# A hybrid decoder block on one core: where a scan's second output tile is finished, the order of its state products, and two output steps ahead of the last states

## The chip, the core and the metric

The kernel runs on one core of a Trainium2 chip. It is timed in device microseconds (us) from start to end of one execution. The core has engines that run side by side, each with its own queue of instructions: TensorE for matrix products (PE in the profile, with PEld for its weight loads), VectorE (DVE), ScalarE (ACT), GpSimd (POOL) and SyncE (SP), which issues most of the transfers from memory. Products land in PSUM, a small memory beside the large SBUF. An engine takes its instructions in their order; where one has to wait for another engine, all that is behind it in its queue waits too.

## What is computed

One layer of a decoder for 512 tokens of width 1024, with 16 learned tokens (the "meta" tokens) put in front. Two branches read the same normalised input: a pooling branch and a Mamba-2 branch, a scan with 8 groups of 4 heads. Each is projected back to width 1024, weighted by a gate of its own, and their sum goes through `w_o` and an MLP with a squared ReLU. The case is about the Mamba-2 branch:

```python
xbc = silu(causal_depthwise_conv(xbc, conv_w, conv_b))      # x, B and C of every group
dt = softplus(dt_raw + dt_bias)
...
cb = einsum("bclgn,bcsgn->bclsg", cf, bf)                   # C against B within a chunk
y_diag = einsum("bclsg,bclsgr,bcsgrp->bclgrp", cb, lmat, xdt)
decay_states = exp(a_cs[:, :, -1:] - a_cs)
states = einsum("bclgn,bclgr,bclgrp->bcgrpn", bf, decay_states, xdt)
# states are carried from chunk to chunk: h = chunk_decay * h + state
y_off = einsum("bclgn,bcgrpn,bclgr->bclgrp", cf, prev, exp(a_cs))
y = y_diag + y_off + xs * d_skip
y = y * silu(z)
y = y * rsqrt(mean(y * y, over the group's 256 channels) + eps) * norm_w
y_ssd = y @ w_ssd_out
h = h + (gate_pool * y_pool + gate_ssd * y_ssd) @ w_o
```

The sequence is cut into chunks of 128 tokens; the 16 meta tokens form a short chunk of their own ahead of the four others.

## The kernel before

**Precision.** Every large product is made of three: each operand is split into a high part (the cast `whi` for weights, L75) and a low part (`wlo`, the difference, L76), and high by high, high by low and low by high are added up. So each block of weights (128 x 1024) costs ScalarE a cast and VectorE a subtraction. `block()` (L81) hands out the next split block and first prepares one more, so that two lie ready ahead during the scans.

**The scan.** A loop runs over the 8 groups; I call the pass for group g round g. Within round g TensorE alternates between the scan of group g and *steps*, which are other products that keep it busy while VectorE and ScalarE work on the scan. In rounds 0 to 3, 5 and 6 the steps are the four projections of the next group's B, C and x (`xbc_tile`, tile `px`, each followed by its convolution `conv`, L344, on ScalarE and VectorE). In round 4 they are eight products of the output projection over the first eight row tiles (`out_half`), and in round 7 eight more over row tiles 8 to 13 (`out_part`, L593, tile `psp`; each is followed by a sum onto `acc` on VectorE, L597). Then, except in round 7, come the two z projections (`z_half`, tile `pz`) and, where `GATE_AT` has an entry (rounds 1, 2, 3 and 6), the product of one gate (`gate_product`, tile `pgp`).

The parts of a scan, in the order in which `scan_with` (L601) issues them:

- `turn`: B and x are turned to token-major by TensorE into PSUM (tiles `ptb`, `ptm`, `ptx`). ScalarE copies B's meta columns to `bm` and the rest to `btok`; VectorE makes the meta rows `xm`, then `xdt` (x times dt), the low part of `bm` (L449) and `xdd` (`xdt` times the decay, L450).
- `steps[0]`, then what is `held` over from the round before, then `spread` (the exponentials `eb`, L457, on ScalarE), then the function that `steps[0]` returned.
- `states`: TensorE makes the chunks' products of C and B (`pcb`, L475) and the four states (`pst`): the one of the meta chunk from `bm` and `xm` (L482), and three from `btok` and `xdd` (L484). ScalarE copies the first; VectorE carries the states on (L488, L489).
- Two more steps, between them `spans`, `decays` (ScalarE turns `abc` into decays) and `scores` (L493: VectorE multiplies `abc` by the masked products).
- `outputs`: TensorE makes `po` (L503) from the carried states and `py` (L509) from `abc` and `xdt`. More steps, `gather` (y, gated by `zt`), `squares`, and the norm's column sums (`png`, L529).

`root` turns the sums into the factor `rs` (ScalarE, L533 and L534). `finish` (L536) then does for each of the two row tiles of the group: y times the norm weight and `rs` on VectorE (L539), a cast to `yh` on ScalarE (L542), the difference `yl` on VectorE (L543), and appends the pair to `ys`, from which the output projection reads.

**Order.** The whole scan stands in a region in which TensorE, ScalarE and VectorE each issue their instructions in the order in which the code emits them. The two lists that matter at the seam of two rounds are `held`, whose entries are called behind `steps[0]` of the next round, and `steps`. At the end of a round without a gate (0, 4 and 5) the SiLU of `zt` is put into `held`; with a gate it is done at once and the gate's sigmoid (L672), which reads `pgp`, is put into `held`. `finish` comes before the next round's `turn`, except in round 4, where it is called within the scan, as in round 7.

**PSUM.** Two pools: `psa` with two buffers of 1024 columns (L59), for `px`, `pz`, `pgp`, `psp` and the like, and `psb` with four of 512 columns. A product into a buffer waits until the last reader of the buffer's former tile is done.

## Time and profile before

| | |
|---|---|
| median of 3 runs | 1022.80 us (1022.66 to 1023.13) |
| the profiled execution | 1022.52 us |
| its span, first to last instruction | 1020.8 us |
| mean granted TensorE clock | 0.997 of full speed |
| TensorE busy | 1003.9 us, 98% of the span |
| VectorE busy | 712.3 us, 70% |
| ScalarE busy | 561.5 us, 55% |
| GpSimd busy | 88.7 us, 9% |

The profile records each instruction with its line in the code, the tile it writes and those it reads, its start and its duration. For idle time it names the instruction that ended it. Matmuls are pipelined and their ends are modelled, so neighbours overlap in the record. Further views give the busy time of each engine in any stretch, with the clock that TensorE was granted in it. Times within the profile count from the start of the span.

### The profile page before, as it was taken

To read this page: it belongs to the slowest core of one execution; us is meant where nothing else is said; L and a number is where in the kernel's file an instruction comes from. 1 tells how busy PE (TensorE), PEld (TensorE's weight loads), DVE (VectorE), ACT (ScalarE), POOL (GpSimd) and SP (SyncE) were. 2 spreads that over 40 slices of the span, in tenths; PEclk is the share of its full clock that TensorE was granted. 3 is DMA by queue.
4 is the path that set the end of the run, shared out by engine and by line. 5 is a ranking of instruction groups with operands and counts; after the bars stand their busy time and mean duration, and the time that the engine had idled before them with its cause. 6 is when DMAs were issued, how large, how long until landed. Compare 5 with 4: busy or idle time off the path is not lost.

```text
span 1020.8 us, 14036 instructions
## 1 busy us (share of the span) xinstructions
PE 1003.9 (98%) x5689; PEld 873.6 (86%) x5689; DVE 712.3 (70%) x894; ACT 561.5 (55%) x789; POOL 88.7 (9%) x52
## 2 busy tenths in 40 slices
PE   9999999999999999999999999999999999999997
PEld 8889889898889998978899888888888888888886
DVE  7978586777645586767765466985776577666865
ACT  7765958595843659494244343474545455354444
POOL 0100000000000000000000001003040431413400
PEclk9999999999999999999999999999999999999999
DMA  6233232323232231323632334133323323324112
GB/s 239 71 139 103 63 121 66 125 76 131 83 124 83 83 105 62 127 83 100 206 103 84 107 101 138 68 107 141 103 81 116 113 83 123 92 95 124 42 42 83
DMA packets 29282, 105.64 MB, mean 103 GB/s; under 512 B 3296, under 2 KB 4256, under 8 KB 28192
## 3 DMA queue, kind: packets, MB, share of 16 engines
q1 hardware_dynamic: 26496, 92.75, 28.4%
q0 software_dynamic: 2000, 11.08, 3.0%
q8 instruction: 45, 0.74, 0.3%
q10 hardware_dynamic: 720, 0.91, 0.2%
q14 instruction: 21, 0.17, 0.1%
HBM read 102.55 MB, written 2.16 MB: 103 GB/s over the span
## 4 chain that ended last, share of the span: by engine, by line
PE 84%; ACT 9%; DVE 6%; issue 1%; DMA 0%; SPq 0%; ACTq 0%
PE pf L100 6%; PE pf L99 6%; PE pf L101 6%; PE px L157 5%; PE px L158 5%; PE px L160 5%; PE alpha L1063 3%; PE alpha L1064 3%; PE alpha L1065 3%; PE pz L160 2%; PE pz L157 2%; PE pz L158 2%; PE py L509 2%; PE pp L160 2%; PE pp L157 1%; ACT whi L75 1%
## 5 line engine op out<-in xcount | busy, mean ns | idle before, releaser
L76 DVE TENSOR_TENSOR wlo<-raw,whi 128x1024 fp32r<-128x1024 f32 (+1 forms) x131 | 163.9, 1253 | 118.8 <-ACT whi L75 118.8
L75 ACT CAST whi<-raw 128x1024 fp32r<-128x1024 f32 (+1 forms) x131 | 136.2, 1041 | 126.7 <-PE pf L100 55.8
L157 PE MATMUL px<-uh,whi 128*128 128x264 f32 (+1 forms) x448 | 120.7, 290 | 0.0
L158 PE MATMUL px<-ul,whi 128*128 128x264 f32 (+1 forms) x448 | 117.9, 284 | 0.0
L99 PE MATMUL pf<-vh,whi 128*128 128x512 f32 x256 | 99.8, 390 | 0.0
L101 PE MATMUL pf<-vh,wlo 128*128 128x512 f32 x256 | 99.6, 389 | 0.0
L100 PE MATMUL pf<-vl,whi 128*128 128x512 f32 x256 | 99.6, 389 | 0.0
L160 PE MATMUL px<-uh,wlo 128*128 128x264 f32 (+1 forms) x448 | 90.6, 284 | 0.0
L157 PEld LDWEIGHTS px<-uh,whi 128*128 128x128 f32 x448 | 85.3, 190 | 1.3 <-issue 1.0
L158 PEld LDWEIGHTS px<-ul,whi 128*128 128x128 f32 x448 | 84.9, 189 | 0.3
L825 DVE TENSOR_TENSOR slo<-b,shi 128x1024 fp32r<-128x1024 f32 x35 | 49.2, 1407 | 31.6 <-ACT shi L824 27.4
L160 PEld LDWEIGHTS px<-uh,wlo 128*128 128x128 f32 x448 | 69.0, 188 | 0.0
L824 ACT CAST shi<-b 128x1024 fp32r<-128x1024 f32 x35 | 36.7, 1049 | 47.3 <-PE pf L100 36.4
L99 PEld LDWEIGHTS pf<-vh,whi 128*128 128x128 f32 x256 | 48.1, 188 | 10.0
L101 PEld LDWEIGHTS pf<-vh,wlo 128*128 128x128 f32 x256 | 48.0, 188 | 10.0
L100 PEld LDWEIGHTS pf<-vl,whi 128*128 128x128 f32 x256 | 48.1, 188 | 9.8
L1074 POOL TENSOR_TENSOR b<-b,b 128x1024 f32<-128x1024 f32 x14 | 35.6, 2542 | 238.4 <-DVE slo L825 238.4
L1063 PE MATMUL alpha<-shi,hh 128*128 128x512 f32 x140 | 54.6, 390 | 0.0
L1065 PE MATMUL alpha<-shi,hl 128*128 128x512 f32 x140 | 54.5, 389 | 0.0
L1064 PE MATMUL alpha<-slo,hh 128*128 128x512 f32 x140 | 54.5, 389 | 0.0
L890 DVE TENSOR_TENSOR ht<-ht,alpha 128x1024 f32<-128x1024 f32 x35 | 42.6, 1218 | 10.9 <-PE alpha L1065 10.9
L347 ACT ACTIVATE xc<-px,vs 128x528 f32<-128x528 f32 x14 | 11.1, 790 | 62.3 <-PE px L160 62.3
(418 smaller groups left out, 2511.8 us busy)
## 6 DMA issues: line engine op xcount, KB each, us to landing
raw<-in_w SPq DMA_DIRECT2D x129, 512.0 KB, 3.6
b<-in_w SPq DMA_DIRECT2D x28, 512.0 KB, 3.6
abc<-acs_d POOLq DMA_DIRECT2D x8, 1024.0 KB, 6.0
wob<-in_w SPq DMA_DIRECT2D x8, 512.0 KB, 5.5
xt<-in_xT SPq DMA_DIRECT2D x8, 264.0 KB, 5.2
ht<-in_x POOLq DMA_DIRECT2D x4, 512.0 KB, 5.5
w<-in_w SPq DMA_DIRECT2D x4, 512.0 KB, 3.5
out_dram<-out SPq DMA_DIRECT2D x4, 320.0 KB, 2.4
```

The costliest lines, as they stand in the source:

```text
L75: act.copy(hi[:, c], raw[:, c])
L76: dve.tensor_tensor(lo[:, c], raw[:, c], hi[:, c].bitcast(F32), op=ALU.subtract)
L99: pe.matmul(ps, ah, bh, start=first, stop=False)
L100: pe.matmul(ps, ah, bl, start=False, stop=False)
L101: pe.matmul(ps, al, bh, start=False, stop=last)
L157: pe.matmul(o, wh, rhs[0][k][:, c], start=k == 0, stop=False)
L158: pe.matmul(o, wh, rhs[1][k][:, c], start=False, stop=False)
L160: pe.matmul(o, wl, rhs[0][k][:, c], start=False, stop=k == NK - 1)
L825: dve.tensor_tensor(lo, src, hi.bitcast(F32), op=ALU.subtract)
L1063: pe.matmul(ps[t], a[0], wh[:, cs], start=f, stop=False, skip_group_check=True)
L1064: pe.matmul(ps[t], a[0], wl[:, cs], start=False, stop=False, skip_group_check=True)
L1065: pe.matmul(ps[t], a[1], wh[:, cs], start=False, stop=l, skip_group_check=True)
```

## The change

- In `turn`, VectorE makes `xdd` ahead of the low part of `bm`.
- In `states`, the product of the meta chunk is issued behind the three others. `pv[0]` and what reads it are the same.
- `finish` takes the tiles that it is to do. At the end of rounds 0 and 5, which have no gate and end with a `finish`, only tile 0 is finished before the next `turn`; tile 1 is put into `held`, behind the SiLU of `zt`. `held` is now emptied from the front.
- In round 7 the first step is two output steps, so output steps 0 and 1 both stand ahead of `held`, `spread` and `states`; the list has seven entries, and the output step that stood between the last sum onto `acc` and `finish` falls away (`steps[7:]` is empty there; in round 4 it has one entry as before).

```diff
             self.xdd = gs.tile([P, 3, R, 64], F32, tag="xdd", name=f"xdd{g}")
+            dve.tensor_tensor(self.xdd, xdt[:, :3, :, :], bc(dec[:, :3, hs], 64), op=ALU.mult)
             dve.tensor_tensor(bm[low], pbm, bm[hi].bitcast(F32), op=ALU.subtract)
-            dve.tensor_tensor(self.xdd, xdt[:, :3, :, :], bc(dec[:, :3, hs], 64), op=ALU.mult)
...
-            pe.matmul(pv[0], bm, flat(xm), start=True, stop=True)
             for c in range(3):
                 pe.matmul(pv[c + 1], btok[:, c, :], xdd[:, c, :, :].rearrange("p r d -> p (r d)"),
                           start=True, stop=True)
+            pe.matmul(pv[0], bm, flat(xm), start=True, stop=True)
             act.copy(flat(st[0]), pv[0])
...
-        def finish(self):
-            for i in range(2):
+        def finish(self, tiles=(0, 1)):
+            for i in tiles:
...
         while held:
-            held.pop()()
+            held.pop(0)()
...
-            steps[7]()()
+            for step in steps[7:]:
+                step()()
             sc.finish()
...
             if g + 1 == G:
-                scan_with(sc, [lambda d=d: out_part(d) for d in range(NK)])
+                def two():
+                    out_part(0)()
+                    return out_part(1)
+
+                scan_with(sc, [two] + [lambda d=d: out_part(d) for d in range(2, NK)])
                 break
...
             if gate is not None:
                 z_silu()
                 pg = gate_product(gate)
+                sc.root()
+                sc.finish()
+                held.append(lambda d=gate, pg=pg: act.activation(m1[d], pg, AF.Sigmoid, bias=col(V_BG, d)))
             else:
                 held.append(z_silu)
-            if g != 4:
-                sc.root()
-                sc.finish()
-            if gate is not None:
-                held.append(lambda d=gate, pg=pg: act.activation(m1[d], pg, AF.Sigmoid, bias=col(V_BG, d)))
+                if g != 4:
+                    sc.root()
+                    sc.finish((0,))
+                    held.append(lambda sc=sc: sc.finish((1,)))
```

## The prediction

> **What bounds the kernel now.** I read the page first, then TensorE's own list of waits, then the timeline of each engine in rounds 1, 2, 6 and 7 (round g is the scan of group g).

> ```profile
> PE 1003.9 (98%) x5689; PEld 873.6 (86%) x5689; DVE 712.3 (70%) x894; ACT 561.5 (55%) x789; POOL 88.7 (9%) x52
> PE pst L482 <- DVE bm L449: 4.4, 3, 1.5
> PE pst L484 <- DVE xdd L450: 3.6, 6, 0.6
> ```

> TensorE is busy for 1003.9 of 1020.8 us. Of what is left, 4.4 + 3.6 = 8.0 us stand in front of the state products (tile `pst`; columns: total, times, longest), and the change goes for these. Whether it gets them depends on what comes next in the same round. Round 1 is the first of the two in which the finish of the second tile moves. TensorE there (start, duration, then in brackets the idle time before it and who ended it):

> ```profile
> 115.88 1.05 PE L475 MATMUL pcb<-ct,bt 128*128 128x128 f32 x8
> 118.46 0.35 PE L482 MATMUL pst<-xm,bm 80*128 80x256 f32 x1 [1.52 <-DVE bm L449]
> 119.45 1.53 PE L484 MATMUL pst<-xdd,btok 128*128 128x256 f32 x6 [0.64 <-DVE xdd L450]
> 120.63 0.47 PE L157 MATMUL px<-uh,whi 128*128 128x258 f32 x1
> 126.54 0.28 PE L157 MATMUL px<-uh,whi 128*128 128x264 f32 x1
> 134.52 2.18 PE L509 MATMUL py<-abc,xdt 128*64 128x128 f32 x32 [0.22 <-ACT whi L75]
> ```

> TensorE loses 1.52 + 0.64 = 2.16 us at `pst`, and yet it waits again, 0.22 us, at `py` (L509). `py` multiplies the decays `abc`, which VectorE's scores (L493) write last:

> ```profile
> 113.15 0.75 DVE L539 SCALAR_TENSOR_TENSOR yt<-yt,vs,rs 128x512 f32<-128x512 f32 x1
> 115.20 0.40 DVE L434 TENSOR_TENSOR xdm<-ptm,decm 16x256 f32<-16x256 f32 x1
> 118.03 0.28 DVE L449 TENSOR_TENSOR bm<-ptb,bm 16x128 fp32r<-16x128 f32 x1
> 118.34 0.96 DVE L450 TENSOR_TENSOR xdd<-xdt,dec 128x768 f32<-128x768 f32 x1
> 119.22 1.22 DVE L76 TENSOR_TENSOR wlo<-raw,whi 128x1024 fp32r<-128x1024 f32 x1
> 123.05 2.37 DVE L350 SCALAR_TENSOR_TENSOR bt<-px,vs,bt 128x527 f32<-128x527 f32 x3 [2.62 <-ACT bt L347]
> 133.20 2.36 DVE L493 TENSOR_TENSOR abc<-abc,cbm 128x1024 f32<-128x1024 f32 x2
> ```

> The first of the two scores ends about 133.20 + 1.18 = 134.38, and `py` starts 0.14 us later. (The wait is put down to a `whi` cast that `py` doesn't read; the scores are what it reads.) From 123.05 to the scores VectorE shows no idle time, so the scores are as early as the convolution L350 at 123.05 lets them be, and that one waited 2.62 us for ScalarE:

> ```profile
> 111.89 0.62 ACT L542 CAST yh<-yt 128x512 fp32r<-128x512 f32 x1 [0.82 <-DVE yt L539]
> 113.93 0.62 ACT L542 CAST yh<-yt 128x512 fp32r<-128x512 f32 x1 [1.42 <-DVE yt L539]
> 117.72 1.02 ACT L661 ACTIVATE zt<-pz 128x1024 f32<-128x1024 f32 x1
> 118.77 1.28 ACT L457 ACT_TABLE_LOAD   x1
> 122.23 0.79 ACT L347 ACTIVATE bt<-px,vs 128x528 f32<-128x528 f32 x1
> ```

> So in round 1 two chains run side by side: TensorE's, with 2.16 us of waits in it, and ScalarE to VectorE to scores to `py`, which is 0.22 us longer still. **The second one sets the end of the round**; the wait at `pst` is time that TensorE would otherwise lose at `py`.

> **The change, part by part**

> *Finish of tile 1 behind the turning (rounds 1 and 6).* VectorE: after `yl` of tile 0 it starts turning (`xdm`) where tile 1's L539 stood, at 113.15 instead of 115.20, 2.05 us earlier. `xdd`, now ahead of the `bm` subtraction, starts at 118.34 - 2.05 - 0.31 = 115.98 and ends at 116.94; the six L484 can start at about 117.1, right behind `pcb`, and the meta product after them (at most 0.35) lets TensorE on at about 118.6 instead of 120.63. That is the 2.0 us gained at `pst`.

> What it costs is on ScalarE. There tile 1's cast `yh` now stands behind the SiLU of `zt` and ahead of the spread (L457). ScalarE saves the wait of 1.42 us and a cast, 113.93 - 111.89 = 2.04 us, so `zt` runs from 115.68 to 116.70. Then it must wait for tile 1's L539, which VectorE reaches only behind the turning and the `wlo` of the next weight block: `wlo` starts at 119.22 - 2.05 = 117.17, takes 1.13 to the next start (1.22 less an overlap of 0.09 between neighbours, as `xdd`'s end and the next start show), L539 runs from 118.30 to 119.05, the cast from 119.08 to 119.70. The table load of the spread, queued behind that cast, starts at 119.73 instead of 118.77: **0.96 us later**. Everything that ScalarE has queued behind it moves by that (`bt` L347, the state copy, `whi`, the spans and decays), VectorE's convolution moves to 124.01, and `py` to 134.52 + 0.96 = 135.48. VectorE has 2.62 us of idle time there, so `yl` of tile 1 costs nothing.

> The 2.0 us of TensorE don't vanish, they move. The next `xbc` tile but one needs the PSUM buffer that the convolution of `bt` reads: it ends at 124.01 + 2.37 = 126.38, so the product at 126.54 stays where it is, with a new wait of about 2.0 us before it; then 0.22 + 0.96 = 1.2 us at `py`. Round 1: **+0.96**, not -2.0.

> *Round 6* has the same instructions, but TensorE was late there for another reason.

> ```profile
> 117.47:120.88 3.41, 1.79 (x8) 1.50 (x9) 2.90 (x4) 3.37 (x4) 0.00 (x0) 1.00 0.00 0
> 393.95:397.36 3.41, 1.24 (x8) 0.85 (x7) 3.32 (x6) 3.38 (x3) 0.00 (x0) 1.00 0.00 0
> 397.36:400.77 3.41, 3.41 (x14) 3.03 (x13) 0.80 (x2) 3.35 (x6) 0.00 (x0) 0.50 0.47 150
> 410.58 2.35 DVE L493 TENSOR_TENSOR abc<-abc,cbm 128x1024 f32<-128x1024 f32 x2
> 413.24 1.97 PE L509 MATMUL py<-abc,xdt 128*64 128x128 f32 x32
> ```

> These are windows (stretch, length, busy time of PE, PEld, DVE, ACT and POOL, then the granted clock). The stretch in which TensorE was busy for 1.24 of 3.41 us was followed by 3.41 us at clock 0.50; the one of round 1 with 1.79 of 3.41 was not. Half a clock over 3.41 us is 1.7 us of matmul time lost. That is why `py` of round 6 started at 413.24, although the scores would have let it start at 410.58 + 1.18 + 0.14 = 411.90. With VectorE 0.96 later it can start at 412.86, and with no stop at `pst` that slow stretch goes: **-0.38**.

> *Meta product last, `xdd` first (all rounds).* The subtraction's 0.31 us leaves the way to `xdd`; the meta product's 0.35 us, until now done while TensorE waited for `xdd`, comes behind. In rounds 2 to 4:

> ```profile
> 168.43 1.53 PE L484 MATMUL pst<-xdd,btok 128*128 128x256 f32 x6 [0.53 <-DVE xdd L450]
> 181.83 2.35 DVE L493 TENSOR_TENSOR abc<-abc,cbm 128x1024 f32<-128x1024 f32 x2
> 183.20 2.13 PE L509 MATMUL py<-abc,xdt 128*64 128x128 f32 x32
> ```

> the scores would let `py` start at 183.15, so even the best case gains 0.05 a round. I take **0** (bounds -0.3 to +0.1 for the three). The state copy on ScalarE stands behind the spread and needs the meta product only then; in rounds 0 and 5 nothing waits at `pst`.

> *Two output steps ahead of the states (round 7).*

> ```profile
> 439.34 0.48 PE L99 MATMUL psp<-yh,whi 128*128 128x512 f32 x1
> 443.55 1.06 PE L475 MATMUL pcb<-ct,bt 128*128 128x128 f32 x8
> 445.94 0.35 PE L482 MATMUL pst<-xm,bm 80*128 80x256 f32 x1 [1.33 <-DVE bm L449]
> 446.93 1.53 PE L484 MATMUL pst<-xdd,btok 128*128 128x256 f32 x6 [0.64 <-DVE xdd L450]
> 458.86 2.18 PE L509 MATMUL py<-abc,xdt 128*64 128x128 f32 x32 [0.42 <-ACT abc L468]
> 460.97 0.50 PE L99 MATMUL psp<-yh,whi 128*128 128x512 f32 x1
> 442.84 1.05 ACT L75 CAST whi<-raw 128x1024 fp32r<-128x1024 f32 x1
> 443.91 1.28 ACT L672 ACT_TABLE_LOAD   x1
> 445.20 0.69 ACT L672 ACTIVATE m<-pgp,vs 128x512 f32<-128x512 f32 x1
> 447.83 0.68 DVE L597 TENSOR_TENSOR acc<-acc,psp 128x512 f32<-128x512 f32 x1
> ```

> An output step takes 443.55 - 439.34 = 4.21 us. One more ahead of `pcb` covers the 1.33 and 0.64 at `pst` and the 0.42 at `py`, 2.39 us of idle time. But its product needs a PSUM buffer of `psa`, which has two. One holds output step 0; the other holds the gate product of round 6 (`pgp`), and its reader, the held sigmoid (L672), is issued only after `steps[0]`, so behind both output steps. Before, output step 1 came long after the sigmoid. Now it comes at 443.55, and on ScalarE it puts its own `whi` (1.06 to the next start) ahead of the sigmoid, which ends at 445.20 + 0.69 + 1.06 = 446.95. **Output step 1 starts at about 447.1**; `pcb`, the states and all of TensorE stand behind it. That is 3.55 us after step 0 gives way at 443.55. Matmuls in a row overlap by some 0.15 us (six L484 of about 0.38 in 1.53), so the profile, which counts a stop from the last one's end, would show 3.4 us of idle time. Against the 2.39 that is +1.0; and as each stop loses that overlap beside its idle time and three stops become one, I take **+0.7**. The other buffer becomes free with the sum L597 of step 0: 447.83 + 0.68 gives 448.5, 1.55 us later. Which of the two is taken the trace of before can't say. That buffers go to whoever finds one free, not in turn, the `pcb` row of round 1 shows: it starts at 115.88, before the last reader of `ptb` (L449) at 118.03. I take the sigmoid's, as it is free first.

> A stop of 3.4 us is longer than the 2.17 us that TensorE stood in 393.95 to 397.36. However the stretches of 3.41 us lie, one holds at least half of it; if they lie as before, the one from 445.15 holds some 2.5 us, and is 25% busy. I take the slow stretch as following: **+1.7**, as nothing behind it in round 7 has slack for it. In round 1 the new wait of 2.0 us leaves 41% busy, between the two cases seen; a slow stretch there would cost 1.7 less the 1.2 that waits at `py` anyway, 0.5, and the same in round 6. I take 0 for these and keep 1.0 for the range.

> [...]

> Behind round 7 the finish comes without an output step ahead of it, but the two pool tiles still stand between it and the products that read its rows, so nothing is added.

> **Sum:** 0.96 - 0.38 + 0 + 0.7 + 1.7 = 2.98. Against the profiled execution's own 1022.52 us (span 1020.8 and 1.7 around it, unchanged) this gives **1025.5 us**. The median of the runs, 1022.8, is 0.28 above the profiled one.

> **The rivals**

> *No slow stretch in round 7*: everything as above, TensorE's stop split between two stretches so that neither is empty enough. 1022.52 + 1.28 = 1023.8. For it: 1.79 of 3.41 busy brought none. Against: the stop is twice as long. 18%.

> *The other buffer*: output step 1 waits for the sum of step 0, 1.55 us more: 1027.0. 14%.

> *No wait for a buffer in round 7* (the other side: faster). If output step 1 finds a free buffer at 443.55, the 2.39 us and three restarts are gained, about -2.7, and no slow stretch arises: 1022.52 + 0.96 - 0.38 - 2.7 = 1020.4. It decides from a wait of less than about 2 us in front of that step. For it: nothing in the rows of before, where the step came after the sigmoid. Against: two buffers, both in use. 8%.

> *The change does what its words say*: the waits at `pst` go and nothing takes their place: -2.0 in round 1, -2.0 in round 6, -2.7 in round 7, 1015.8. For it: the rows of waits. Against: the scores, which set `py` in round 1 to within 0.14 us. 4%.

> *Slow stretches in rounds 1 and 6 as well*: 1026.5. 8%. My own sum keeps 48%.

> **How the numbers follow.** A measurement of this kernel can tell about 0.2% from no change, 2.05 us: below 1020.75 is faster, above 1024.85 slower. Slower gets my case (48%), the other buffer and the further slow stretches, less some 7% for terms that come out smaller: 63%. Same gets the first rival and these: 27%. Faster gets the two on the other side, less their near misses: 10%. The range runs from 1023.3 (the first rival, with 0.5 less) to 1027.7 (the other buffer and some of a further slow stretch).

> **What the profile after would show.** In rounds 1 and 6 no idle time at `pst`, but about 2 us in front of the `xbc` product that follows the convolution of `bt`, and over 1 us at `py`; the spread's table load about 1 us later behind tile 1's cast. In rounds 2 to 4 the meta product behind the six, and `py` where it was. In round 7 no wait at `pst` and `py`, but one of over 3 us in front of the second output step, ended by ScalarE's sigmoid, and a stretch of 3.41 us at clock 0.50 behind it. I am wrong if that second step starts right behind the first, or if `py` of round 1 comes earlier than it did.

## The result, and the profile after

The changed kernel takes 1025.62 us (median of 11 runs, 1024.09 to 1027.78), the kernel before 1023.46 us (11 runs, 1022.66 to 1024.15). The ratio is 1.0023, with a 95% interval of 1.0014 to 1.0032: slower by 1.4 to 3.3 us. The prediction was 1025.5.

The list of TensorE's waits after the change (total, times, longest) shows what became of the 8.0 us at `pst`:

```profile
PE px L157 <- DVE bt L350: 4.4, 2, 2.2
PE psp L99 <- ACT m L673: 3.2, 1, 3.2
PE pst L483 <- DVE xdd L449: 1.7, 5, 0.7
PE py L509 <- ACT whi L75: 1.1, 1, 1.1
```

At `pst` 6.3 us are gone; 4.4 us stand in front of two `xbc` products, 3.2 in front of an output step, 1.1 at `py`. The first two of these rows weren't there before; `py` had 0.2 us behind `whi` and 0.4 behind `abc`. TensorE's timeline says where. I measure a round from its turning (L424) to `py` (L509), and round 7 to its fifth output step (step 4), the first that both kernels issue behind the same work. The kernel before, from its timeline (`py` stands in the prediction):

```profile
108.54 0.49 PE L424 MATMUL ptb<-ident,bt 128*128 128x128 f32 x3
385.92 0.49 PE L424 MATMUL ptb<-ident,bt 128*128 128x128 f32 x3
437.90 0.49 PE L424 MATMUL ptb<-ident,bt 128*128 128x128 f32 x3
465.18 0.39 PE L99 MATMUL psp<-yh,whi 128*128 128x512 f32 x1
```

The changed kernel, same view. Round 1:

```profile
108.76 0.49 PE L424 MATMUL ptb<-ident,bt 128*128 128x128 f32 x3
117.33 1.53 PE L483 MATMUL pst<-xdd,btok 128*128 128x256 f32 x6 [0.17 <-DVE xdd L449]
126.89 0.36 PE L157 MATMUL px<-uh,whi 128*128 128x264 f32 x1 [2.19 <-DVE bt L350]
136.21 1.97 PE L509 MATMUL py<-abc,xdt 128*64 128x128 f32 x32
```

Round 6:

```profile
387.21 0.49 PE L424 MATMUL ptb<-ident,bt 128*128 128x128 f32 x3
405.36 0.36 PE L157 MATMUL px<-uh,whi 128*128 128x264 f32 x1 [2.19 <-DVE bt L350]
414.30 2.18 PE L509 MATMUL py<-abc,xdt 128*64 128x128 f32 x32 [1.10 <-ACT whi L75]
```

Round 7:

```profile
439.17 0.49 PE L424 MATMUL ptb<-ident,bt 128*128 128x128 f32 x3
448.18 0.50 PE L99 MATMUL psp<-yh,whi 128*128 128x512 f32 x1 [3.20 <-ACT m L673]
468.28 0.50 PE L99 MATMUL psp<-yh,whi 128*128 128x512 f32 x1
```

| stretch | before | after | difference |
|---|---|---|---|
| round 1, turning to `py` | 25.98 | 27.45 | +1.47 |
| round 6, turning to `py` | 27.32 | 27.09 | -0.23 |
| round 7, turning to output step 4 | 27.28 | 29.11 | +1.83 |

The three make +3.07; the spans differ by 1023.7 - 1020.8 = 2.9. The rest of the rounds isn't quite equal: from `py` of round 1 to the next turning the changed kernel takes 24.65 us for 24.86, in round 6 24.87 for 24.65, and round 4 is 0.2 us shorter. Behind output step 4 both take 549.5 us to the end of TensorE's work. (The times of these two executions differ by more, 4.1: what lies outside the span was 1.7 us in the one and 3.0 in the other.)

In round 1 the six state products start 8.57 us behind the turning, where they started 10.91 behind it, and the product at 126.89 has lost that again. ScalarE's timeline of round 1 shows by what:

```profile
115.92 1.03 ACT L666 ACTIVATE zt<-pz 128x1024 f32<-128x1024 f32 x1
119.45 0.62 ACT L542 CAST yh<-yt 128x512 fp32r<-128x512 f32 x1 [2.50 <-DVE yt L539]
120.09 1.28 ACT L457 ACT_TABLE_LOAD   x1
```

The SiLU is 2 us earlier, then ScalarE stands for 2.50 us before the cast of tile 1, and the spread behind it comes 11.33 us after the turning, 10.23 before the change (118.77 - 108.54). ScalarE in round 7, where the sigmoid (L673) now stands behind two `whi` (its table load lies in between):

```profile
444.13 1.99 ACT L75 CAST whi<-raw 128x1024 fp32r<-128x1024 f32 x2
447.44 0.69 ACT L673 ACTIVATE m<-pgp,vs 128x512 f32<-128x512 f32 x1
```

It ends at 448.13, and output step 1 starts at 448.18. (The sum that empties the buffer of output step 0 starts only at 449.24.) The windows of the changed kernel (stretch and length, busy time of PE, PEld, DVE, ACT and POOL, granted clock, transfers):

```profile
124.99:128.40 3.41, 1.50 (x12) 1.54 (x13) 3.20 (x7) 3.38 (x10) 0.00 (x0) 1.00 0.00 0
128.40:131.81 3.41, 3.41 (x18) 3.41 (x17) 3.24 (x6) 3.41 (x8) 0.00 (x0) 0.50 0.02 5
401.47:404.88 3.41, 1.70 (x15) 1.49 (x13) 1.97 (x3) 3.38 (x8) 0.00 (x0) 1.00 0.00 0
445.84:449.25 3.41, 1.07 (x5) 0.90 (x6) 3.31 (x6) 3.36 (x4) 0.00 (x0) 1.00 0.00 0
449.25:452.67 3.42, 3.42 (x10) 2.68 (x9) 1.81 (x3) 2.29 (x3) 0.00 (x0) 0.50 0.58 158
```

Two stretches at clock 0.50, behind the new waits of rounds 1 and 7; before there was one, in round 6, which is gone. In round 6 the new wait was as long as in round 1 (2.19), but the stretch around it kept 1.70 us of busy time and no slow one followed.

### The profile page after: what moved, and what is told of

It reads as the page before. It is cut to its first block, busy times and chain, and to the rows that moved or that the text cites. A ratio compares the mean times of both kernels' runs of the same rounds, so it can differ in the third digit from the quotient of the medians.

```text
span 1023.7 us, 14027 instructions
## 1 busy us (share of the span) xinstructions
PE 1005.2 (98%) x5689; PEld 875.2 (85%) x5689; DVE 713.3 (70%) x894; ACT 561.3 (55%) x789; POOL 88.7 (9%) x52
## 3 DMA queue, kind: packets, MB, share of 16 engines
HBM read 102.55 MB, written 2.16 MB: 102 GB/s over the span
## 4 chain that ended last, share of the span: by engine, by line
PE 84%; ACT 8%; DVE 6%; issue 1%; DMA 0%; SPq 0%; ACTq 0%
PE pf L100 6%; PE pf L99 6%; PE pf L101 6%; PE px L157 5%; PE px L158 4%; PE px L160 4%; PE alpha L1070 3%; PE alpha L1071 3%; PE alpha L1072 3%; PE pz L160 2%; PE pz L157 2%; PE pz L158 2%; PE py L509 2%; PE pp L160 1%; PE pp L158 1%; PE pp L157 1%
## 5 line engine op out<-in xcount | busy, mean ns | idle before, releaser
L76 DVE TENSOR_TENSOR wlo<-raw,whi 128x1024 fp32r<-128x1024 f32 (+1 forms) x131 | 163.9, 1253 | 112.8 <-ACT whi L75 112.6
L75 ACT CAST whi<-raw 128x1024 fp32r<-128x1024 f32 (+1 forms) x131 | 136.0, 1041 | 123.9 <-PE pf L100 55.8
L157 PE MATMUL px<-uh,whi 128*128 128x264 f32 (+1 forms) x448 | 120.1, 289 | 4.4 <-DVE bt L350 4.4
L99 PE MATMUL pf<-vh,whi 128*128 128x512 f32 x256 | 99.9, 390 | 0.0
L157 PEld LDWEIGHTS px<-uh,whi 128*128 128x128 f32 x448 | 85.7, 191 | 6.0 <-ACT abc L463 4.7
L99 PEld LDWEIGHTS pf<-vh,whi 128*128 128x128 f32 x256 | 48.1, 188 | 10.0
L347 ACT ACTIVATE xc<-px,vs 128x528 f32<-128x528 f32 x14 | 11.1, 791 | 61.1 <-PE px L160 61.1
```

The lines of the kernel that those rows point to most:

```text
L75: act.copy(hi[:, c], raw[:, c])
L76: dve.tensor_tensor(lo[:, c], raw[:, c], hi[:, c].bitcast(F32), op=ALU.subtract)
L99: pe.matmul(ps, ah, bh, start=first, stop=False)
L157: pe.matmul(o, wh, rhs[0][k][:, c], start=k == 0, stop=False)
```

## The experiments

The theory: `py` of rounds 1 and 6 follows ScalarE's queue by way of the scores, and output step 1 of round 7 waits for the gate product's PSUM buffer. The rival: TensorE's stops at `pst` are what costs, and the loss comes from one place alone. Each kernel was timed beside the kernel before on the same chip.

### Without the two output steps

```diff
-                def two():
-                    out_part(0)()
-                    return out_part(1)
-
-                scan_with(sc, [two] + [lambda d=d: out_part(d) for d in range(2, NK)])
+                scan_with(sc, [lambda d=d: out_part(d) for d in range(NK)])
```

> The changed kernel, but round 7 with its output steps as before (only output step 0 ahead of the states). Theory (the scores' chain sets py in rounds 1 and 6, a PSUM buffer holds up round 7): rounds 1 and 6 look as in the changed kernel, with about 2.2 us of idle time before the xbc product behind the convolution of bt and over 1 us at py (less where a stretch at clock 0.50 lies in between); from the turning to py of round 1 26.9 to 27.5 us, 25.98 in the kernel before. The 3.2 us of idle time at the second output step and the slow stretch behind it are gone. Time +0.3 to +1.6 us against the kernel before, ratio 1.0003 to 1.0016. Rival (round 7 is not to blame): the ratio stays at the changed kernel's 1.0023.

1023.96 us against 1023.42, ratio 1.0007 (0.9998 to 1.0016): inside what the theory expects and below the rival's 1.0023, though the interval also holds no change. TensorE in round 1:

```profile
109.01 0.49 PE L424 MATMUL ptb<-ident,bt 128*128 128x128 f32 x3
117.57 1.53 PE L483 MATMUL pst<-xdd,btok 128*128 128x256 f32 x6 [0.17 <-DVE xdd L449]
127.13 0.36 PE L157 MATMUL px<-uh,whi 128*128 128x264 f32 x1 [2.18 <-DVE bt L350]
136.08 2.18 PE L509 MATMUL py<-abc,xdt 128*64 128x128 f32 x32 [1.11 <-ACT whi L75]
```

No slow stretch fell into this round here, so this is the bare effect: 27.07 us to `py`, +1.09, and the two waits of 2.18 and 1.11 us in the places named. `py` starts 1.32 us behind the start of the scores (L493, at 134.76), as in the kernel before (134.52 - 133.20), so they still set it. In its round 6 a slow stretch followed the wait (27.37 us to `py`, from the same view). So the moved finish costs a little over 1 us a round where neither kernel has a slow stretch, and a slow stretch there adds 0.3 to 0.4 at `py`: by estimate it costs 1.7 us of matmul time (half a clock over 3.41 us), and 1.11 of that fall into the wait at `py`, which isn't there in these two rounds. With the finish as before, a slow stretch costs such a round more: 27.32 us to `py` in round 6 of the kernel before, and 27.23 and 27.31 in round 1 of the next two kernels, against 25.98. Compared with these the moved finish costs next to nothing, which fits that the whole kernel is 0.54 us slower by the medians and not 2.2.

### The two output steps alone

```diff
-            steps[7]()()
+            for step in steps[7:]:
+                step()()
...
-                scan_with(sc, [lambda d=d: out_part(d) for d in range(NK)])
+                def two():
+                    out_part(0)()
+                    return out_part(1)
+
+                scan_with(sc, [two] + [lambda d=d: out_part(d) for d in range(2, NK)])
```

> The kernel before with only the two output steps ahead of round 7's states. Theory: about 3.2 us of idle time in front of output step 1, ended by the sigmoid, no idle time at pst and py of round 7, and mostly a stretch at clock 0.50 behind it. From the turning of round 7 to the output step behind py and output steps 1 and 2, one step more done: net +0.7 us, with the slow stretch +2.4. Ratio 1.0007 to 1.0024. Rival (the steps cover the waits, rounds 1 and 6 alone cost the time): -2.4 us or more, ratio below 0.998.

1024.52 us against 1023.42, ratio 1.0015 (1.0006 to 1.0023): the theory's range, against the rival's below 0.998. TensorE in round 7, and the windows around its wait:

```profile
438.11 0.49 PE L424 MATMUL ptb<-ident,bt 128*128 128x128 f32 x3
447.09 0.50 PE L99 MATMUL psp<-yh,whi 128*128 128x512 f32 x1 [3.18 <-ACT m L677]
465.59 0.50 PE L99 MATMUL psp<-yh,whi 128*128 128x512 f32 x1
```

```profile
441.93:445.35 3.42, 1.98 (x9) 1.31 (x7) 2.95 (x7) 3.38 (x7) 0.00 (x0) 1.00 0.00 0
445.35:448.76 3.41, 1.67 (x7) 1.41 (x8) 3.35 (x6) 3.37 (x4) 0.00 (x0) 1.00 0.00 0
```

The wait is the same as in the changed kernel, 3.18 us, but it fell almost evenly into two stretches (1.98 and 1.67 us busy), and no slow one followed: 27.48 us from the turning to output step 4. That is the bare price of the step, +0.20 against 27.28. With the slow stretch of the changed kernel it was 29.11, 1.63 more. The profiled execution is one of the two fastest of this kernel (1022.74 us, where the runs go from 1022.62 to 1026.48). The mean granted clock on record is 0.997 for these two and 0.991 to 0.996 for the other nine, so most executions spent more time below full clock, and the traces show no lower clock than 0.50; where they spent it isn't shown.

### The buffer given free earlier

The sigmoid of round 6's gate, which empties `pgp`, goes between the two casts of round 6's finish, where ScalarE waited 1.42 us.

```diff
                 act.copy(yh, y)
+                if i == 0 and between:
+                    between()
...
+            sig = None
+            if gate is not None:
+                sig = lambda d=gate, pg=pg: act.activation(m1[d], pg, AF.Sigmoid, bias=col(V_BG, d))
             if g != 4:
                 sc.root()
-                sc.finish()
-            if gate is not None:
-                held.append(lambda d=gate, pg=pg: act.activation(m1[d], pg, AF.Sigmoid, bias=col(V_BG, d)))
+                sc.finish(sig if g == 6 else None)
+            if gate is not None and g != 6:
+                held.append(sig)
```

This is on the kernel with only the two output steps.

> As the kernel with only the two output steps, but the sigmoid of round 6's gate is issued on ScalarE between the two casts of round 6's finish, so that the gate product's PSUM buffer is free before output step 1. Theory (the buffer): the idle time in front of output step 1 goes to below 0.3 us, no idle time at pst and py of round 7, no slow stretch; -2.4 to -2.9 us against the kernel before, ratio 0.9970 to 0.9978. Rival (something else holds up output step 1, its weights or the sum of output step 0): over 2 us of idle time stay in front of it, ratio above 0.9995.

1019.62 us against 1023.42, ratio 0.9967 (0.9954 to 0.9979), a little more than the 0.9970 to 0.9978 that were expected, and far from the rival's 0.9995. TensorE and ScalarE:

```profile
437.80 0.49 PE L424 MATMUL ptb<-ident,bt 128*128 128x128 f32 x3
443.75 0.40 PE L99 MATMUL psp<-yh,whi 128*128 128x512 f32 x1
462.12 0.50 PE L99 MATMUL psp<-yh,whi 128*128 128x512 f32 x1
```

```profile
441.21 0.69 ACT L677 ACTIVATE m<-pgp,vs 128x512 f32<-128x512 f32 x1
```

The sigmoid ends at 441.90; at 443.75 output step 1 runs with no idle time in front of it, and output step 4 comes 24.32 us behind the turning, 2.96 less than before. Only the sigmoid changed its place in the order; the weights and sums of the output steps kept theirs. So the buffer it was, and the two steps are worth 3 us once it is free. (The early sigmoid without the two steps wasn't run; what it would bring by itself, at the 0.42 us of `py`, is not shown.)

### The order of the state products alone

```diff
+            dve.tensor_tensor(self.xdd, xdt[:, :3, :, :], bc(dec[:, :3, hs], 64), op=ALU.mult)
             dve.tensor_tensor(bm[low], pbm, bm[hi].bitcast(F32), op=ALU.subtract)
-            dve.tensor_tensor(self.xdd, xdt[:, :3, :, :], bc(dec[:, :3, hs], 64), op=ALU.mult)
...
-            pe.matmul(pv[0], bm, flat(xm), start=True, stop=True)
             for c in range(3):
...
+            pe.matmul(pv[0], bm, flat(xm), start=True, stop=True)
```

> The kernel before with only xdd ahead of the low part of bm and the meta product behind the three others. Theory: in rounds 1, 6 and 7 one wait at pst instead of two, about 0.3 us shorter in all; in rounds 2 and 3 the idle time at pst goes from 0.5 to 0.35 and py stays within 0.1 us of its place; 0 to -0.5 us in all, ratio 0.9995 to 1.0002. Rival (the waits at pst count in full): -0.3 us in each of seven rounds, -2 us, ratio 0.998.

1022.43 us against 1023.42, ratio 0.9993 (0.9984 to 1.0002): too close to tell from nothing (from 1.6 us faster to 0.2 slower), and the rival's 0.998 lies just outside the interval. TensorE in round 1:

```profile
109.02 0.49 PE L424 MATMUL ptb<-ident,bt 128*128 128x128 f32 x3
119.62 1.53 PE L483 MATMUL pst<-xdd,btok 128*128 128x256 f32 x6 [2.21 <-DVE xdd L449]
134.99 2.18 PE L509 MATMUL py<-abc,xdt 128*64 128x128 f32 x32 [0.39 <-ACT whi L75]
```

Two waits at `pst` became one of 2.21 us; the products start 0.31 us earlier against the turning, and `py` comes at 25.97, where it came at 25.98: what is won at `pst` is waited for at `py`. Beside the further kernels below it was tried the other way round as well:

> The kernel with all three (multiplication ahead of the turning, sigmoid between the casts, two output steps ahead), but with the low part of bm ahead of xdd and the meta product first, as in the kernel before. Theory (the order of the state products is worth next to nothing, since the scores follow ScalarE): two waits at pst again in rounds 1 and 6, together about 0.2 us longer than the 0.83 of the other order; py of round 1 24.4 to 24.7 us behind the turning; ratio within 0.0006 of the 0.9924 of the kernel with the meta product last. Rival: with ScalarE ahead, TensorE's waits at pst set the rounds, and the time is 1 us or more above that kernel's, ratio 0.9934 or more.

1015.13 us, ratio 0.9921 (0.9908 to 0.9935), where its twin with the meta product last has 0.9924 (0.9910 to 0.9937). So no pair of kernels shows an effect of the order that stands out of the noise.

### ScalarE's cast ahead of the SiLU

```diff
         while held:
-            held.pop(0)()
+            held.pop()()
```

This is on the kernel without the two output steps.

> The changed kernel with round 7's output steps as before and held emptied from the back, so that ScalarE's cast of tile 1 stands ahead of the SiLU of zt and not behind it. Theory (py of rounds 1 and 6 follows ScalarE's queue): the SiLU and the spread wait with it; the spread's table load comes about 3.3 us later than in the kernel before, py of round 1 about 29.3 us behind the turning (25.98 before, 27.07 with the SiLU first), round 6 the same; about +5 to +7 us on the kernel before. Rival (what counts is when TensorE passes pst): as with the SiLU first, +0.5 us, since the turning and pst keep their places.

1029.24 us against 1023.42 (two runs), ratio 1.0057 (1.0039 to 1.0075). TensorE and ScalarE in round 1:

```profile
108.61 0.49 PE L424 MATMUL ptb<-ident,bt 128*128 128x128 f32 x3
117.19 1.53 PE L483 MATMUL pst<-xdd,btok 128*128 128x256 f32 x6 [0.17 <-DVE xdd L449]
122.31 0.58 PE L157 MATMUL px<-uh,whi 128*128 128x258 f32 x1 [3.47 <-ACT zt L662]
138.50 1.97 PE L509 MATMUL py<-abc,xdt 128*64 128x128 f32 x32
```

```profile
119.31 0.62 ACT L542 CAST yh<-yt 128x512 fp32r<-128x512 f32 x1 [4.85 <-DVE yt L539]
122.28 1.28 ACT L457 ACT_TABLE_LOAD   x1
```

VectorE's scores:

```profile
136.70 2.35 DVE L493 TENSOR_TENSOR abc<-abc,cbm 128x1024 f32<-128x1024 f32 x2
```

The turning and `pst` keep their places to 0.02 us, and `py` comes 29.89 us behind the turning, 3.9 later than before; ScalarE's spread comes 3.4 later (13.67). TensorE's stop has wandered once more, to the product whose buffer the late SiLU has to empty. This is the plainest sign that `pst` doesn't set the round. It doesn't show that the scores do: there is no wait in front of `py` here, and it starts 1.80 us behind the scores' start and not 1.32, so they would have let it start at about 29.4, near the 29.3 that was expected. What makes TensorE later still is that stop of 3.47 us and the 6.83 us at clock 0.50 behind it. Both ways lead back to ScalarE's queue, the one by the scores, the other by the SiLU's buffer.

### Tile 1's multiplication ahead of the turning

If the queue sets the round, the cast must not wait. So VectorE's multiplication (L539) of tile 1 stays ahead of the turning, and only cast and difference are held (`weigh` is that line of `finish` as a function of its own).

```diff
                     sc.finish((0,))
-                    held.append(lambda sc=sc: sc.finish((1,)))
+                    sc.weigh(1)
+                    held.append(lambda sc=sc: sc.finish((1,), False))
```

This too is on the kernel without the two output steps.

> The changed kernel with round 7's output steps as before, and in rounds 1 and 6 tile 1's multiplication (L539) on VectorE ahead of the turning; its cast and difference stay held behind the SiLU. Theory: ScalarE's cast then waits for nothing, so the spread starts some 1.5 us earlier than in the kernel before, while pst keeps about 0.8 of its 2.2 us of idle time; py of round 1 and 6 about 24.5 us behind the turning (25.98 before). -3 us for the two, ratio 0.9960 to 0.9980 with fewer slow stretches. Rival (TensorE's waits at pst set the round): about 0.7 us a round worse than the changed kernel at pst, ratio 1.000 or above.

1018.42 us against 1023.42, ratio 0.9953 (0.9941 to 0.9966), more than the 0.9960 to 0.9980 that were expected, and not the rival's 1.000. TensorE, VectorE's scores and ScalarE in round 1:

```profile
108.77 0.49 PE L424 MATMUL ptb<-ident,bt 128*128 128x128 f32 x3
117.99 1.53 PE L483 MATMUL pst<-xdd,btok 128*128 128x256 f32 x6 [0.83 <-DVE xdd L449]
133.22 2.18 PE L509 MATMUL py<-abc,xdt 128*64 128x128 f32 x32 [0.26 <-ACT whi L75]
131.90 2.35 DVE L493 TENSOR_TENSOR abc<-abc,cbm 128x1024 f32<-128x1024 f32 x2
```

```profile
115.92 1.02 ACT L667 ACTIVATE zt<-pz 128x1024 f32<-128x1024 f32 x1
116.84 0.61 ACT L547 CAST yh<-yt 128x512 fp32r<-128x512 f32 x1
117.47 1.28 ACT L457 ACT_TABLE_LOAD   x1
```

The cast follows the SiLU at once. TensorE waits longer at `pst` than in the changed kernel (0.83 for 0.17 us), and `py` comes 24.45 us behind the turning, 2.6 us earlier than in the kernel without the two steps, and again 1.32 us behind the start of the scores. A longer stop at `pst` and yet an earlier `py`: this shows that the way over ScalarE and the scores sets the round. No stretch at clock 0.50 is left between round 1 and round 7; the mean granted clock is 0.999. The gain of 5 us is more than the 3 us of the two rounds (1.5 each). The rest fits slow stretches that no longer come: the mean granted clock is 0.998 on average over the runs of this kernel and 0.996 over those of the kernel before, which by estimate is 2 us of the 1020.

### Together

Multiplication ahead of the turning, sigmoid between the casts, two output steps ahead:

> Tile 1's multiplication ahead of the turning with its cast held (rounds 0 and 5), the sigmoid of round 6's gate between the two casts, two output steps ahead of round 7's states, meta product last. Theory: the gains add up, -3 us and -2.9 us, ratio 0.9930 to 0.9950, no idle time over 1 us from round 1 to round 7 at pst, px, psp or py except in round 4. Rival: TensorE is held up elsewhere (weight casts, DMA) and the sum is less than 4 us.

1015.45 us against 1023.42, ratio 0.9924 (0.9910 to 0.9937), a gain of about 8 us, more than the 0.9930 to 0.9950 that were expected: within the intervals the two gains, 3.8 and 5.0, add up. With the same split of the finish in the gated rounds 1 and 2:

> As the kernel with all of these, and the same split of the finish (multiplication ahead of the turning, cast held behind the gate's sigmoid) in the gated rounds 1 and 2. Theory: pst of rounds 2 and 3 loses its 0.35 to 0.5 us, the spread comes earlier too, so py follows; another -0.5 to -1.0 us, ratio 0.9922 to 0.9945. Rival: the sum of step 0 or the cast ahead of the spread holds py, no gain on the kernel with all of these.

1013.78 us, ratio 0.9907 (0.9893 to 0.9920), and in the round after the gated round 1:

```profile
158.85 0.49 PE L424 MATMUL ptb<-ident,bt 128*128 128x128 f32 x3
181.91 1.97 PE L509 MATMUL py<-abc,xdt 128*64 128x128 f32 x32
```

23.06 us from the turning to `py`, with no wait at either place (23.82 before). It gains 1.7 us more, where up to 1.0 was expected. The two intervals don't separate that, but the traces show it: from this turning to the next round 2 takes 47.72 us, 48.65 in the kernel with all three, and round 3 is 0.9 shorter too. This is the fastest of all kernels run here, some 12 us faster than the changed one.

## Why the prediction was right, point by point

- **The number.** That 1025.5 comes so near to the median of 1025.62 is in part luck. The sum started from an execution of 1022.52 us, and the median of the kernel before is 1023.46; the change was put at +2.98 and is +2.16 by the medians. These two misses cancel. The terms as measured in the profiled executions add up to 3.07, but there, too, round 1 is 0.5 above its term and the two output steps with their slow stretch 0.6 below theirs. The mechanisms behind the terms are the ones that were forecast.
- **The wait moves to the `xbc` product and `py` (rounds 1 and 6).** Predicted: idle time of about 2.0 and 1.2 us there and `py` 0.96 us later. Measured without a slow stretch: 2.18, 1.11 and +1.09, with 0.17 left at `pst` where none was forecast. What I missed is that VectorE reached L539 a little later; ScalarE stood for 2.50 us before the cast, where the sum has 119.08 - 116.70 = 2.38.
- **Round 6.** Predicted -0.38, measured -0.23, with the slow stretch of before gone as said. This term is one of the profiled execution alone: in the kernel with only the two output steps round 6 had no slow stretch and took 25.98 us to `py`, as round 1 did in the kernel before. Like against like, round 6 loses as much as round 1.
- **Order of the state products.** Predicted 0, and nothing outside the noise in two pairs of kernels; the traces show 0.2 us gained in round 4 and nothing in rounds 2 and 3, within the bounds given.
- **Two output steps.** The wait for `pgp`'s buffer was predicted at 3.4 us of idle time and was 3.20. The net +0.7 was too large: the kernel with this alone shows +0.20. Of the 0.5 between them 0.2 is the wait itself. The other 0.3 is left to what three stops cost beside their idle time, for which I had 0.3 in all; no run measures that alone. That it is the sigmoid's buffer and not the one of output step 0 (the rival 1.55 us later) the end of the wait shows, 0.05 us behind the sigmoid and ahead of the sum.
- **The slow stretch.** Predicted 1.7; the changed kernel's round 7 took 1.63 more than the same work without it. It is a matter of where the wait falls: in the changed kernel 2.34 of the 3.20 us lay in one stretch (445.84 to 448.18), which was 1.07 us busy, and the slow one came; in the kernel with only the two steps 3.18 us left two stretches 1.98 and 1.67 us busy, and it didn't come. My rival without it was thus right for some executions, and round 1 had one that I had left to the range. Runs of the changed kernel spread over 3.7 us, those before over 1.5. I read this as more or fewer such stretches. The mean granted clock of each run fits that (0.997 in the three runs of the changed kernel up to 1024.56 us, 0.991 to 0.996 in the others), but up to 1.3 us of the spread lies outside the span.
- **The rival on the other side** (a free buffer at output step 1) had its price about right: with the buffer given free the step gains 2.96 us in its round, where it had -2.7.
- **Behind round 7** nothing was to be added for the finish without a step ahead of it, and nothing was: the 549.5 us above.

## What to carry to other kernels

A stop of the busiest engine is worth only what the next meeting point lets through: follow the other engines' queues from the stop to where they meet again, and price the stop by the chain that arrives last (in round 1, without a slow stretch, 2.16 us of idle time at `pst` became 0.17, and `py` came 1.09 us later). Before something is put into another place in a queue that is issued in order, ask what its input waits for there, and what is queued behind it (the cast of tile 1 waited 2.50 us, and the spread behind it came 1.10 later). A step that is moved ahead also needs its buffer earlier: look for the reader that must empty it, and whether that is issued in front of the step or behind (3.20 us of idle time with the sigmoid behind output step 1, none with it in front).
